# Third PSUM bank, tied inverse products, weight parts in four pieces and the norm behind the next preparation, in a block of RWKV7 and gated attention

## Chip, cores and metric

One core of a Trainium2 chip runs the whole block. Five engines work side by side, each on its own queue of instructions, in order: TensorE multiplies matrices, VectorE and ScalarE work on elements and move results out of PSUM, GpSimd does elementwise work from SBUF, and SyncE issues most of the DMA transfers. The metric is the device time of one execution in microseconds, and less is better.

## What is computed

A sequence of 1024 tokens of width 1024 is normalized and projected; a third of the columns feeds an RWKV7 mixer with 8 heads of 64 (a recurrence over time, a norm of its output per head, a gate), a third feeds causal attention with 8 heads of 64 and a forget bias, and the rest are two gates. Both results are projected, gated, added, projected again, and normalized.

```python
def reference(x, norm_g, w_in, ..., w_out_a, w_out_b, w_out, final_norm_g):
    h = _rmsnorm(x, norm_g[l])
    u = h @ w_in[l]
    u_a, u_b, u_g = jnp.split(u, [RWKV_COLS, RWKV_COLS + FOX_COLS], axis=-1)
    y_a = _rwkv7_mixer(u_a, ...) @ w_out_a[l]
    y_b = _fox_mixer(u_b, ...) @ w_out_b[l]
    g_a, g_b = jnp.split(u_g, 2, axis=-1)
    merged = jax.nn.sigmoid(g_a) * y_a + jax.nn.sigmoid(g_b) * y_b
    x = x + merged @ w_out[l]
    return _rmsnorm(x, final_norm_g)

# in _rwkv7_mixer
    state = (state * w_t[:, :, None, :] + sa[..., None] * b_t[:, :, None, :]
             + v_t[..., None] * k_t[:, :, None, :])          # one step, sa = state @ a_t
    y = (y - mean) * lax.rsqrt(var + LNX_EPS)                # per head
    y = y * lnx_w + lnx_b
    return (y + bonus) * jax.nn.silu(gate)

# in _fox_mixer
    logits = qb @ kp * scale + cum_q - cum_k                 # causal, softmax, times v
    return o * jax.nn.silu(gate)
```

## The kernel before

Every large product is made of three: an operand is split into a part that TensorE's fast fp32 format holds (the H half) and the rest (the L half), and H·H, H·L and L·H are summed. A weight part of 128x1024 is loaded, ScalarE casts it to wH, and GpSimd subtracts, wL = w - wH, in one instruction (split_w, L203 to L206). project (L307 to L313) makes a 128x512 tile of a projection in 8 steps over k of three matmuls each. mix and gate_tile (L322, L351) evacuate such a tile with ScalarE and VectorE: a scaled copy, a shifted combination with the neighbouring token, and the last column kept as last_k and the like.

The program runs through these stages: x is loaded, normalized and transposed (to about 25 us); the projections of r, k, v and of the low-rank inputs for head pairs 0 and 1; then four units, (p, n) = (0,0), (0,1), (1,0), (1,1), each of four heads and half of the sequence. A unit has a preparation, prep, and a chain. prep makes the products of a chunk of 64 tokens (psc, pk and others), inverts triangular matrices by elimination of 32x32 blocks on VectorE (L639, L643, some 30 us), writes them out to DRAM as td and reads them back as Tb, transposes blocks on VectorE (TW, L655), and combines them with two sets of 32 small products on TensorE (pw at L661, pz at L669). chain runs over 8 chunks of time, px, pu and po, with a state that is passed from chunk to chunk, then py (L734) for each four chunks, the norm over the heads (VectorE, L746 to L756), the transposes pt (L761), a scaled copy yo on ScalarE, a product with the gate yg on GpSimd (L771), and a store to yab in DRAM. Behind the four units comes the attention in four pairs of heads: scores sc (L994), softmax on VectorE and ScalarE, transposes pt (L1018), po (L1038). The scores of a pair need qk projected (project_qk), normed and transposed (norm_qk: pqk, pqq, KA, QA), and a copy of parts of QA to other partitions by DMA (L959, L960). At the end merge multiplies y of both mixers by their output weights (pma, pmb) and by the gates.

The order on each engine is made by a list scheduler from priorities: a tile framework takes what was written first unless order(offset) moves its priority. chain and attend run at -LATER, so ahead of all else that is ready. bulky() puts work at +LATER, and that is what fills TensorE meanwhile: the projections of pairs 2 and 3, 24 gate tiles (fill, 48 matmuls of 128x512 each), project_qk, project_v. RFILL, FPRE and FFILL say how many gates may be placed in each of the four units, and ahead of and behind the qk projection in each attention pair. A scheduled order is fixed at build time, and each engine then follows it and waits where an operand is late.

PSUM has eight banks: "pj" 2 (projections), "misc" 2, "aux", "late", "xus" and "y" 1 each (py). Tiles of one tag get its banks in the order in which they are written in the program: a later tile waits until an earlier one has been read, however their priorities stand. ps_misc gives a tile of "misc", ps_pj one of the tags in bulk_tags.

Of the kernel before, what the change touches and what calls it, by code (L numbers as in the profile page):

```python
# [9 lines left out]
F32 = mybir.dt.float32  # L10
# [40 lines left out]
QNB = 1  # L51
QKFIRST = True
LATER = 1000000
PACE = 0.3
PHPOOL = True
APACE = 0
APACE0 = 0.0
FTAGS = ["pj", "pj", "aux"]
TTAGS = ["pj", "misc", "aux", "pj", "misc", "late", "xus"]
PQTAG = ["late", "xus"]  # L60
# [2 lines left out]
NORMPOOL = (0,)  # L63
HSPLIT = 1
HDVE = 0
LSPLIT = 1
PACE0 = 0.0
WA1 = 0
MGB = 3
NQEARLY = True  # L70
ATTFIRST = True
T1B = 3
RFILL = [5, 6, 6, 2]
FPRE = [1, 1, 2, 0]
# [16 lines left out]
def kernel(  # L91
# [6 lines left out]
    nc = tc.nc  # L98
# [9 lines left out]
    bulk_tags = ["pj"]  # L108
# [195 lines left out]
    transposed(1, range(KD))  # L304
    xctx.close()

    def project(ps, wH, wL, rH, rL, n, nk=KD):  # L307

        ts_ = slice(n * HALF, (n + 1) * HALF)
        for k in range(nk):  # L310
            nc.tensor.matmul(ps, wH[:, k, :], rH[:, k, ts_], start=(k == 0), stop=False)  # L311
            nc.tensor.matmul(ps, wH[:, k, :], rL[:, k, ts_], start=False, stop=False)  # L312
            nc.tensor.matmul(ps, wL[:, k, :], rH[:, k, ts_], start=False, stop=(k == nk - 1))  # L313

    yab = dp.tile([8, P, S], F32, tag="yab", name="yab", bufs=1)
    gab = dp.tile([24, P, S], F32, tag="gab", name="gab", bufs=1)
# [76 lines left out]
    HB = 32  # L393
# [84 lines left out]
    def prep(pp_, n):  # L478
# [174 lines left out]
        for e, _, q1, q2 in half:  # L653
            for h in range(2):
                nc.vector.transpose(TW[q1, UC * h : UC * h + UC, :], Tg[q1, h, :, q1])  # L655
        pw = ps_misc(f"pw{u}")
        for h in range(2):
            for c in range(UC):
                g = UC * h + c
                for e, _, q1, q2 in half:  # L660
                    nc.tensor.matmul(pw[q2, g * HB : (g + 1) * HB], Tb[q1, c, h, q2], TW[q1, g, :], start=True, stop=True)  # L661
# [10 lines left out]
        return dict(AR=AR, Q=Q, BKt=BKt, SV=SV, AK=AK, WC=WC, bV=bV, s2c=s2c, lnw=lnw)  # L672

    states = [rp.tile([P, 2, 2, C], F32, tag=f"state{j}", name=f"state{j}") for j in range(2)]
    for t in states:
# [2 lines left out]
    def chain(pp_, n, d):  # L678
# [4 lines left out]
        for c in range(UC):  # L683
            gc = UC * n + c
            st_c, st_n = states[gc % 2], states[1 - gc % 2]
            xs = rp.tile([P, P], F32, tag="xs", name=f"xs{u}_{c}", bufs=2)
            if gc == 0:
                nc.vector.tensor_copy(xs, AK[:, 0])
                nc.gpsimd.memset(yv[:, 0], 0.0)
            else:  # L690

                px = ps_aux(f"px{u}_{c}")
                for e, own, other in pairs:
                    nc.tensor.matmul(
                        px[:, e * P : (e + 1) * P], AR[:, e, c, :], st_c[:, e].rearrange("p h i -> p (h i)"),
                        start=True, stop=True,
                    )
                for e, own, other in pairs:
                    nc.vector.tensor_add(xs[own], px[own, e * P : (e + 1) * P], AK[own, c])
                for e, own, other in pairs:  # L700
                    nc.scalar.copy(yv[own, c].rearrange("p h i -> p (h i)"), px[other, e * P : (e + 1) * P])
                if gc < NCH - 1:
                    ws = rp.tile([P, 2, C], F32, tag="ws", name=f"ws{u}_{c}", bufs=2)
                    for e in range(2):
                        for h, q in ((0, A), (1, B)):
                            nc.scalar.activation(ws[q, e], st_c[q, e, h, :], AF.Copy, scale=WC[q, e, c : c + 1])  # L706
            pu = ps_misc(f"pu{u}_{c}", "late")
            for h in range(2):
                nc.tensor.matmul(pu[:, h * C : (h + 1) * C], Tb[:, c, h, :], xs[:, h * C : (h + 1) * C], start=True, stop=True)
            for e, own, other in pairs:  # L710
                nc.vector.tensor_mul(
                    SV[own, e, c].rearrange("p (h i) -> p h i", h=2),
                    pu[own, 0:P].rearrange("p (h i) -> p h i", h=2),
                    s2c[own, c, :].unsqueeze(2).broadcast_to([64, 2, C]),
                )
            if gc < NCH - 1:
                po = pp.tile([P, HALF], F32, tag="xus", name=f"po{u}_{c}")
                for e, own, other in pairs:
                    nc.tensor.matmul(po[:, e * P : (e + 1) * P], BKt[:, e, c, :], SV[:, e, c, :], start=True, stop=True)
                for e, own, other in pairs:  # L720
                    for h, q in ((0, A), (1, B)):
                        o = po[q, e * P + h * C : e * P + (h + 1) * C]
                        if gc == 0:
                            nc.vector.tensor_scalar(st_n[q, e, h, :], o, WC[q, e, 0:1], None, op0=ALU.mult)
                        else:
                            nc.vector.scalar_tensor_tensor(  # L726
                                st_n[q, e, h, :], o, WC[q, e, c : c + 1], ws[q, e], op0=ALU.mult, op1=ALU.add
                            )
            if c % 4 == 3:
                py = pp.tile([P, HALF], F32, tag="y", name=f"py{u}_{c}").rearrange("p (c h i) -> p c h i", h=2, i=C)  # L730
                for c_ in range(c - 3, c + 1):
                    for h in range(2):
                        for e, own, other in pairs:
                            nc.tensor.matmul(  # L734
                                py[own, c_ % 4, h, :], Q[:, e, h, c_, :], SV[:, e, c_, h * C : (h + 1) * C],
                                start=True, stop=True,
                            )
                yc = yv[:, c - 3 : c + 1]
                nc.vector.tensor_add(yc, yc, py)


        G = 2 * UC
        st = rp.tile([P, 4, G], F32, tag="st", name=f"stat{u}")
        mean, var, rstd, tmp4 = (st[:, j, :] for j in range(4))
# [59 lines left out]
    def project_v(cb):  # L804
# [25 lines left out]
        for b in range(8):  # L830
            bs = slice(b * P, (b + 1) * P)
            pv = ps_pj(f"pfv{cb}_{b}")
            o = pv[:, :ncol]
            for k in range(KD):
                wH, wL = parts[k // KH]
                kk = k % KH
                nc.tensor.matmul(o, hTH[:, k, bs], wH[:, kk, :], start=(k == 0), stop=False)
                nc.tensor.matmul(o, hTH[:, k, bs], wL[:, kk, :], start=False, stop=False)
                nc.tensor.matmul(o, hTL[:, k, bs], wH[:, kk, :], start=False, stop=(k == KD - 1))
# [40 lines left out]
    def project_qk(p):  # L880
# [17 lines left out]
        for n in range(2):  # L898
            xt = fpa[0].tile([P, 4, QB], F32, tag="xn", name=f"xn{p}_{n}", bufs=2)
            rs = fpa[0].tile([P, 3, 16], F32, tag="rs", name=f"rs{p}_{n}", bufs=2)  # L900
            for b in range(4):
                bs = slice((4 * n + b) * P, (4 * n + b + 1) * P)
                ps = ps_pj(f"pf{p}_{n}_{b}")[:, :QB]
                for k in range(KD):
                    wH, wL = parts_[k // KH]
                    kk = k % KH
                    nc.tensor.matmul(ps, hTH[:, k, bs], wH[:, kk, :], start=(k == 0), stop=False)  # L907
                    nc.tensor.matmul(ps, hTH[:, k, bs], wL[:, kk, :], start=False, stop=False)  # L908
                    nc.tensor.matmul(ps, hTL[:, k, bs], wH[:, kk, :], start=False, stop=(k == KD - 1))  # L909
# [14 lines left out]
    def norm_qk(p, xn, rr):  # L924
# [10 lines left out]
        for n in range(2):  # L935
            xg = xn[n].rearrange("p b (g i) -> p (b g) i", i=HD)
            (nc.gpsimd if n in NORMPOOL else nc.vector).tensor_mul(xg, xg, rr[n].unsqueeze(2).broadcast_to([P, 16, HD]))
            for c, key in ((1, "k"), (0, "q")):
# [15 lines left out]
                        )  # L954
                if key == "q":
                    nc.sync.dma_start(qlo[:, HS[n]], ql.bitcast(F32))
            if n == 1:
                QAf = QA.bitcast(F32)
                nc.sync.dma_start(QAf[B, 0, :], QAf[A, 0, :])  # L959
                nc.sync.dma_start(QAf[A, 1, :], QAf[B, 1, :])  # L960
        return KA, QA, qlo, cb

    sc_tags = SCTAGS
# [146 lines left out]
        return mH, mL, [(w[:, 0], w[:, 1]) for w in wo]  # L1110

    units = [(p, n) for p in range(2) for n in range(2)]
    for p in range(2):
        proj_rkv(p)
        if p == 0:
            for p_ in range(NP):
                lora(p_)
    for i, (p, n) in enumerate(units):
        d = prep(p, n)
        if i + 1 == len(units):  # L1120
            open_early()
        with bulky():
            if i == 0:
                proj_rkv(2)
                proj_rkv(3)
            fill(RFILL[i], 0)
            if i + 1 == len(units):
                qk = project_qk(0)
                project_v(0)
                forget()  # L1130
        with order(-LATER):
            chain(p, n, d)
    open_late()
    bulk_tags[:] = FTAGS
    qk = norm_qk(0, *qk)
# [94 lines left out]
```

## Time and profile before

| | |
|---|---|
| median of 3 runs | 1168.89 us (1167.12 to 1171.15) |
| profiled execution, its own time | 1171.96 us |
| its span in the trace | 1170.3 us |
| mean granted clock of TensorE in it | 0.973 |
| TensorE busy | 1064.0 us, 91% of the span |
| VectorE busy | 725.5 us, 62% |
| ScalarE busy | 459.7 us, 39% |
| GpSimd busy | 284.8 us, 24% |

The busy times of the page say which engine is the scarcest. Its idle time is then looked up in the list of waits, which names the instruction that waited and what released it; the timeline of an engine shows a place instruction by instruction; and windows give busy time and granted clock of a stretch, 1.0 being 2.4 GHz and 0.5 being 1.2 GHz. Matmuls overlap in the trace, so the distance of their starts, not their length, says what one costs.

### The profile page before, as it was taken

How to read it: one execution, taken by the hardware profiler on the slowest of the kernel's cores; microseconds unless marked ns; L12 is line 12 of the kernel's file. 1: busy time of each engine (PE TensorE's matmuls, PEld its weight loads, DVE VectorE, ACT ScalarE, POOL GpSimd, SP SyncE). 2: the span in 40 equal slices, each digit the busy share in tenths (PEclk: the TensorE clock that was granted, in tenths of full speed). 3: DMA queues.
4: the chain of work that ended last, by engine and by line, in shares of the span. 5: the costliest groups of instructions: out<-in, count | busy, mean ns of one | idle time of the engine just before them, and what ended most of it. 6: DMA issues, size and time to landing. Idle time of an engine off the chain costs nothing. (4 is left out here: it accounts for less than half of the span.)

```text
span 1170.3 us, 18157 instructions
## 1 busy us (share of the span) xinstructions
PE 1064.0 (91%) x6591; PEld 873.6 (75%) x6591; DVE 725.5 (62%) x1855; ACT 459.7 (39%) x969; POOL 284.8 (24%) x296
## 2 busy tenths in 40 slices
PE   3897998999989898999989979999989788999997
PEld 3676775867768776777888878887968766877886
DVE  7514676588745866386847449686377577466145
ACT  5534232434224331443233346554355355232222
POOL 4420320125110341114201222313222211251400
PEclk9998999999999998999999989999999899999999
DMA  6156434124341343213311151423142150663223
GB/s 207 48 158 211 131 81 114 55 90 123 101 113 46 119 118 108 64 55 83 92 28 38 41 177 42 122 59 91 36 140 86 43 165 19 203 205 114 95 91 126
DMA packets 126043, 118.20 MB, mean 101 GB/s; under 512 B 33361, under 2 KB 91842, under 8 KB 125954
## 3 DMA queue, kind: packets, MB, share of 16 engines
q1 hardware_dynamic: 113664, 94.99, 27.8%
q10 hardware_dynamic: 11714, 21.52, 5.0%
q8 instruction: 52, 0.85, 0.3%
q0 software_dynamic: 576, 0.54, 0.2%
q14 instruction: 37, 0.30, 0.1%
HBM read 79.23 MB, written 35.68 MB: 98 GB/s over the span
## 5 line engine op out<-in xcount | busy, mean ns | idle before, releaser
L311 PE MATMUL ps_gg<-hTH,wH_gg 128*128 128x512 f32 x384 | 158.5, 413 | 3.3 <-DVE gt L338 2.2
L313 PE MATMUL ps_gg<-hTH,wL_gg 128*128 128x512 f32 x384 | 159.4, 415 | 0.0
L312 PE MATMUL ps_gg<-hTL,wH_gg 128*128 128x512 f32 x384 | 157.9, 411 | 0.0
L206 POOL TENSOR_TENSOR wL_gg<-w_gg,wH_gg 128x1024 fp32r<-128x1024 f32 x24 | 60.2, 2508 | 269.6 <-ACT wH_gg L203 263.2
L311 PEld LDWEIGHTS ps_gg<-hTH,wH_gg 128*128 128x128 f32 x384 | 73.4, 191 | 19.3 <-DVE gt L338 3.0
L313 PEld LDWEIGHTS ps_gg<-hTH,wL_gg 128*128 128x128 f32 x384 | 73.9, 192 | 14.6
L312 PEld LDWEIGHTS ps_gg<-hTL,wH_gg 128*128 128x128 f32 x384 | 73.5, 191 | 13.5
L907 PE MATMUL pf<-wqkH,hTH 128*128 128x256 f32 x256 | 74.7, 292 | 0.0
L908 PE MATMUL pf<-wqkL,hTH 128*128 128x256 f32 x256 | 74.7, 292 | 0.0
L909 PE MATMUL pf<-wqkH,hTL 128*128 128x256 f32 x256 | 74.7, 292 | 0.0
L376 ACT ACTIVATE gt<-ps_gg 128x512 f32<-128x512 f32 x40 | 23.9, 598 | 99.9 <-PE ps_gg L313 89.3
L1005 ACT ACTIVATE pr<-pr,mm 128x128 f32<-128x128 f32 (+3 forms) x64 | 49.9, 780 | 28.3 <-DVE mm L1001 27.4
L639 DVE TENSOR_TENSOR etmp<-lt 64x30 f32<-64x30 f32 (+14 forms) x120 | 51.4, 429 | 10.9 <-issue 7.3
L1183 PE MATMUL pz<-wo,mH 128*128 128x512 f32 (+1 forms) x136 | 53.1, 390 | 2.9 <-ACT mH L1092 2.9
L706 ACT ACTIVATE ws<-state,WC 64x64 f32<-64x64 f32 x112 | 38.7, 345 | 40.2 <-DVE state L726 33.5
L1185 PE MATMUL pz<-wo,mL 128*128 128x512 f32 (+1 forms) x136 | 52.6, 387 | 0.0
L1018 PE MATMUL pt<-ident,pr 128*128 128x128 f32 x288 | 48.2, 275 | 4.4 <-DVE pr L1009 4.4
L1184 PE MATMUL pz<-wo,mH 128*128 128x512 f32 (+1 forms) x136 | 52.2, 384 | 0.0
L908 PEld LDWEIGHTS pf<-wqkL,hTH 128*128 128x128 f32 x256 | 49.9, 195 | 0.5
L907 PEld LDWEIGHTS pf<-wqkH,hTH 128*128 128x128 f32 x256 | 49.9, 195 | 0.2
L909 PEld LDWEIGHTS pf<-wqkH,hTL 128*128 128x128 f32 x256 | 49.9, 195 | 0.2
L643 DVE TENSOR_TENSOR lt<-lt,etmp 64x30 f32<-64x30 f32 (+14 forms) x120 | 46.7, 390 | 3.8
(333 smaller groups left out, 2829.5 us busy)
## 6 DMA issues: line engine op xcount, KB each, us to landing
w_gg<-in_w_in_dram SPq DMA_DIRECT2D x24, 512.0 KB, 3.7
gab<-gt ACTq DMA_DIRECT2D x48, 256.0 KB, 2.1
xt<-in_x_dram SPq DMA_DIRECT2D x8, 512.0 KB, 5.8
wqk<-in_w_in_dram SPq DMA_DIRECT2D x16, 256.0 KB, 3.3
cb<-cumd SPq DMA_DIRECT2D x8, 512.0 KB, 5.4
yt<-yab SPq DMA_DIRECT2D x16, 256.0 KB, 3.4
ta<-gab SPq DMA_DIRECT2D x16, 256.0 KB, 3.5
wot<-in_w_out_dram SPq DMA_DIRECT2D x16, 256.0 KB, 2.9
```

The source lines that it names most:

```text
L206: nc.gpsimd.tensor_sub(wL[:, k], w[:, k], wH[:, k])
L311: nc.tensor.matmul(ps, wH[:, k, :], rH[:, k, ts_], start=(k == 0), stop=False)
L312: nc.tensor.matmul(ps, wH[:, k, :], rL[:, k, ts_], start=False, stop=False)
L313: nc.tensor.matmul(ps, wL[:, k, :], rH[:, k, ts_], start=False, stop=(k == nk - 1))
L639: nc.vector.tensor_mul(tm, lt3[:, s, s + 1 :].unsqueeze(1).broadcast_to([4 * NG, s, m]), lt3[:, :s, s].unsqueeze(2).broadcast_to([4 * NG, ...
L907: nc.tensor.matmul(ps, hTH[:, k, bs], wH[:, kk, :], start=(k == 0), stop=False)
L908: nc.tensor.matmul(ps, hTH[:, k, bs], wL[:, kk, :], start=False, stop=False)
L909: nc.tensor.matmul(ps, hTL[:, k, bs], wH[:, kk, :], start=False, stop=(k == KD - 1))
L1005: nc.scalar.activation(pr[:, :w], pr[:, :w], AF.Exp, bias=last, scale=-1.0, accum_out=mm[:, 2:3])
L1183: nc.tensor.matmul(ps, mH[:, k, bs], oH[:, k, c], start=(k == 0), stop=False)
L1184: nc.tensor.matmul(ps, mH[:, k, bs], oL[:, k, c], start=False, stop=False)
L1185: nc.tensor.matmul(ps, mL[:, k, bs], oH[:, k, c], start=False, stop=(k == KD - 1))
```

## The change

Six things change.

1. The norm is taken out of chain and becomes norm_out. It runs at order(LATER // 2) for the first three units and at -LATER for the last.
2. The 32 products pw of each unit are tied by not_before to a place among the projections: laid() counts the third matmul of each step over k, and pw of a unit may stand on TensorE only behind the one with the number in PLACE. The tie orders TensorE's queue and has no semaphore.
3. Projections in the RWKV part have three banks, "pj" twice and "y"; py goes from "y" to "misc", and its 16 products are issued in one block behind the last po or pu of its chunks.
4. A weight part's subtraction on GpSimd is made in four pieces of 128x256 (LSPLIT).
5. The gates move: 20 instead of 19 in the RWKV part, and in the attention pairs 0, 1, 1 and 2 instead of 2, 3, 0 and 0.
6. The copies of QA are made for each half of the sequence (four of 128 KB instead of two of 256 KB).

```diff
-LSPLIT = 1
+LSPLIT = 4
-RFILL = [5, 6, 6, 2]
-FPRE = [1, 1, 2, 0]
-FFILL = [1, 3, 2, 0]
+RFILL = [5, 6, 5, 4]
+FPRE = [0, 0, 1, 2]
+FFILL = [0, 1, 0, 0]
+PLACE = {"pw0_0": 179, "pw0_1": 307, "pw1_0": 424, "pw1_1": 540}
+RTAGS = ["pj", "pj", "y"]
...
+    def laid(ins):
+        laid_.append(ins.ins)
+
+    def not_before(first, name):
+        if name not in PLACE:
+            return
+        for ins in first:
+            tc.add_manual_dep(
+                ins, laid_[PLACE[name]].name,
+                mybir.DependencyInfo(mybir.DependencyClass.NoSync, mybir.DependencyReason.DATA),
+                reason="not_before",
+            )
...
-            nc.tensor.matmul(ps, wL[:, k, :], rH[:, k, ts_], start=False, stop=(k == nk - 1))
+            laid(nc.tensor.matmul(ps, wL[:, k, :], rH[:, k, ts_], start=False, stop=(k == nk - 1)))
...
             if c % 4 == 3:
-                py = pp.tile([P, HALF], F32, tag="y", name=f"py{u}_{c}")...
+                py = pp.tile([P, HALF], F32, tag="misc", name=f"py{u}_{c}", bufs=2)...
+                with tc.issue_after(last_mm.ins):
                     ...
                 nc.vector.tensor_add(yc, yc, py)
+        return yv
+
+    def norm_out(pp_, n, d, yv):
...
-            if n == 1:
-                QAf = QA.bitcast(F32)
-                nc.sync.dma_start(QAf[B, 0, :], QAf[A, 0, :])
-                nc.sync.dma_start(QAf[A, 1, :], QAf[B, 1, :])
+            QAf = QA.bitcast(F32)[:, :, HS[n]]
+            nc.sync.dma_start(QAf[B, 0], QAf[A, 0])
+            nc.sync.dma_start(QAf[A, 1], QAf[B, 1])
...
+    bulk_tags[:] = RTAGS
...
+        not_before(d["pw"], f"pw{p}_{n}")
         with order(-LATER):
-            chain(p, n, d)
+            yv = chain(p, n, d)
+        with order(LATER // 2 if i + 1 < len(units) else -LATER):
+            norm_out(p, n, d, yv)
```

How this moves instructions is shown at three places. The first is TensorE at the end of unit 0's preparation, before. pw are the products on the inverse's blocks, ps_k and ps_r tiles of projections of pairs 2 and 3.

```order
L313 MATMUL ps_k_1627<-hTH,wL_k_1589 128x512
L661 MATMUL pw_0_1308<-TW_0_1303,Tb 32x32
L311 MATMUL ps_k_1627<-hTH,wH_k_1588 128x512
...
L311 MATMUL ps_k_1627<-hTH,wH_k_1588 128x512
L661 MATMUL pw_0_1308<-TW_0_1303,Tb 32x32 x16
L312 MATMUL ps_k_1627<-hTL,wH_k_1588 128x512
...
L661 MATMUL pw_0_1308<-TW_0_1303,Tb 32x32 x15
L311 MATMUL ps_r_1664<-hTH,wH_r_1658 128x512
```

The first product pw stands alone, 13 projection matmuls later follow 16 more and then 15. After the change, at the same place:

```order
L329 MATMUL ps_r_1700<-hTH,wH_r_1691 128x512
L330 MATMUL ps_r_1700<-hTL,wH_r_1691 128x512
L331 MATMUL ps_r_1700<-hTH,wL_r_1692 128x512
L681 MATMUL pw_0_1329<-TW_0_1324,Tb 32x32 x32
L329 MATMUL ps_r_1700<-hTH,wH_r_1691 128x512
L330 MATMUL ps_r_1700<-hTL,wH_r_1691 128x512
```

All 32 stand in one block, and further back: 27 projection matmuls later, counted from pk; in the other units 21, 29 and 4 later.

The second place is TensorE at the end of the last unit, before: py_1_7 is the second half of that unit's y, pcs and pct belong to forget's running sum, pt_1_0 and pt_1_1 are the transposes behind the norm, and sc_0 are the first scores.

```order
L734 MATMUL py_1_7_5913<-SV_1_4608,Q_1_4605 64x64
L838 MATMUL pfv_2_5498<-wvL_0_5425,hTH 128x264
L734 MATMUL py_1_7_5913<-SV_1_4608,Q_1_4605 64x64 x3
L941 MATMUL pqq_0_5999<-ident,xn_0_5162 128x128 x4
...
L866 MATMUL pcs<-lf,tri 128x64
L867 MATMUL pcs<-lf,tri 128x64
...
L875 MATMUL pct<-ident,run 64x128
L761 MATMUL pt_1_0_5954<-ident,yv_1_5706 128x128 x4
...
L761 MATMUL pt_1_1_5961<-ident,yv_1_5706 128x128 x4
...
L994 MATMUL sc_0_0_0_0_6043<-KA_5983,QA_5984 128x256
```

py stood among the values' projections pfv, 160 rows ahead of pcs, and some 125 rows lay between pt and the scores. After the change:

```order
L937 MATMUL pf_0_2_6828<-wqkH_0_6748,hTL 128x256
L903 MATMUL pct<-ident,run 64x128
L758 MATMUL py_1_3_5980<-SV_1_4633,Q_1_4630 64x64 x16
L758 MATMUL py_1_7_6086<-SV_1_4633,Q_1_4630 64x64 x16
...
L935 MATMUL pf_1_2_6958<-wqkH_0_6748,hTH 128x256
L789 MATMUL pt_1_0_6127<-ident,yv_1_5879 128x128 x4
L789 MATMUL pt_1_1_6134<-ident,yv_1_5879 128x128 x4
...
L937 MATMUL pf_1_2_6958<-wqkH_1_6758,hTL 128x256
L969 MATMUL pqk_1_6186<-ident,xn_1_5459 128x128 x4
L969 MATMUL pqq_1_6195<-ident,xn_1_5459 128x128 x4
L1021 MATMUL sc_0_0_0_0_6218<-KA_6156,QA_6157 128x256
```

Both halves of y stand behind pct now, 98 qk matmuls pf lie between them and pt, and pqk, pqq and the scores follow pt by 17 more.

The third place is SyncE's queue ahead of attention 0, before. yab<-yo_1 are the stores of the last unit's output, yg loads of gates, cb the broadcast of the forget sums, QA<-QA the copies that the scores wait for.

```order
L772 DMA yab<-yo_1_5953 128x512
L770 DMA yg_1_1_5972<-gab 128x512
L772 DMA yab<-yo_1_5953 128x512
L821 DMA wv_0_7025<-in_w_in_dram 128x4x256
L976 DMA yg_0_6039<-gab 128x256
L934 DMA cb_5986<-cumd 128x1024 x2
L1052 DMA yt_0_9736<-yab 128x512
L956 DMA qlo_5985<-ql_0_6006 128x512
L959 DMA QA_5984<-QA_5984 64x1024
L960 DMA QA_5984<-QA_5984 64x1024
L973 DMA QZ_0_6033<-qlo_5985 64x256 x2
```

After the change:

```order
L800 DMA yab<-yo_1_6126 128x512
L798 DMA yg_1_1_6145<-gab 128x512
L800 DMA yab<-yo_1_6126 128x512
L1003 DMA yg_0_6214<-gab 128x256
L962 DMA cb_6159<-cumd 128x1024 x2
L986 DMA QA_6157<-QA_6157 64x512
L984 DMA qlo_6158<-ql_0_6179 128x512
L987 DMA QA_6157<-QA_6157 64x512
L986 DMA QA_6157<-QA_6157 64x512
L987 DMA QA_6157<-QA_6157 64x512
```

The copies come in four, and the first still stands behind both stores of yo_1, a load of yg and cb; the load yt of the merge is no longer among them.

## Rows read from the trace of the kernel before

**Rows 1.** The page: busy time, share of the span and instructions of each engine.

```profile
PE 1064.0 (91%) x6591; PEld 873.6 (75%) x6591; DVE 725.5 (62%) x1855; ACT 459.7 (39%) x969; POOL 284.8 (24%) x296
```

**Rows 2.** TensorE's waits: line <- what it waited for: total us, times, longest.

```profile
PE pw L661 <- DVE TW L655: 14.9, 4, 4.2
...
PE ps_r L311 <- DVE last_k L344: 8.6, 2, 5.2
...
PE sc L994 <- DMA QA<-QA: 7.0, 2, 6.2
...
PE pt L761 <- DVE yv L756: 5.3, 3, 3.1
...
PE pma L312 <- DVE ya L1054: 4.1, 3, 1.8
...
PE pma L311 <- ACT ya L1053: 3.0, 1, 3.0
...
PE pv L506 <- DVE bon L609: 2.3, 1, 2.3
```

**Rows 3.** Windows: length; busy PE, PEld, DVE, ACT, POOL; granted clock; DMA share; GB/s.

```profile
99.00:111.00 12.00, 6.76 (x17) 5.12 (x18) 5.00 (x11) 4.28 (x7) 2.36 (x1) 0.72 0.48 176
...
457.00:470.00 13.00, 8.77 (x56) 6.13 (x54) 3.00 (x6) 1.53 (x2) 0.68 (x1) 0.74 0.58 151
...
692.20:752.50 60.30, 58.57 (x382) 51.32 (x383) 44.32 (x132) 32.91 (x81) 16.93 (x30) 0.96 0.29 88
...
925.00:945.30 20.30, 13.25 (x44) 9.58 (x43) 16.31 (x30) 10.58 (x18) 2.64 (x1) 0.75 0.43 131
...
945.30:999.90 54.60, 47.89 (x281) 37.44 (x280) 41.64 (x120) 28.61 (x70) 11.55 (x23) 1.00 0.25 82
```

**Rows 4.** Timeline of TensorE around pw of unit 0: start, length, instruction, wait ahead.

```profile
190.91 0.40 PE L312 MATMUL ps_k<-hTL,wH_k 128*128 128x512 f32 x1
...
191.14 0.40 PE L313 MATMUL ps_k<-hTH,wL_k 128*128 128x512 f32 x1
...
195.20 0.24 PE L661 MATMUL pw<-TW,Tb 32*32 32x32 f32 x2 [3.66 <-DVE TW L655]
...
196.54 0.63 PE L311 MATMUL ps_k<-hTH,wH_k 128*128 128x512 f32 x1
...
196.97 0.63 PE L312 MATMUL ps_k<-hTL,wH_k 128*128 128x512 f32 x1
```

**Rows 5.** Timeline of VectorE, end of unit 0's elimination, same columns.

```profile
184.29 2.36 DVE L639 TENSOR_TENSOR etmp<-lt 64x108 f32<-64x108 f32 x1
...
186.69 0.26 DVE L643 TENSOR_TENSOR lt<-lt,etmp 64x108 f32<-64x108 f32 x1
...
194.71 0.43 DVE L655 STREAM_TRANSPOSE TW<-Tb 32x256 f32<-32x256 f32 x1 [0.63 <-DMA Tb<-td]
```

**Rows 6.** GpSimd: one weight part in the timeline; a group (busy, mean ns, idle before).

```profile
184.13 2.40 POOL L206 TENSOR_TENSOR wL_v<-w_v,wH_v 128x1024 fp32r<-128x1024 f32 x1 [10.33 <-ACT wH_v L203]
...
L1042 POOL TENSOR_TENSOR yo<-yo,yg 128x256 f32<-128x256 f32 x16 | 14.5, 908 | 36.3 <-DVE yo L1041 35.4 <-POOL QZ L972 0.9
```

**Rows 7.** Timeline of SyncE's queue ahead of attention 0: issue, length, transfer.

```profile
677.24 0.32 SPq L772 DMA_DIRECT2D yab<-yo  x1
...
683.52 1.25 SPq L959 DMA_DIRECT2D QA<-QA  x1
```

**Rows 8.** Timeline of VectorE, norm of the last unit: its first and last operations.

```profile
640.02 0.69 DVE L739 TENSOR_TENSOR yv<-yv,py 128x512 f32<-128x512 f32 x1 [0.36 <-PE py L734]
...
651.36 1.22 DVE L756 TENSOR_TENSOR yv<-yv,bV 128x1024 f32<-128x1024 f32 x1
```

**Rows 9.** Timeline of TensorE, last unit's pt and qk matmuls behind it.

```profile
667.70 0.66 PE L761 MATMUL pt<-ident,yv 128*128 128x128 f32 x4 [1.00 <-ACT cT L877]
...
672.86 0.28 PE L907 MATMUL pf<-wqkH,hTH 128*128 128x256 f32 x1
...
672.98 0.28 PE L908 MATMUL pf<-wqkL,hTH 128*128 128x256 f32 x1
```

More of the change, by code (lines that the diff above doesn't have):

```diff
@@ L305 @@
     xctx.close()
+    laid_ = []
+    def laid(ins):
[9 more added lines that the diff above has]
+            )
     def project(ps, wH, wL, rH, rL, n, nk=KD):
@@ L656, in prep @@
         pw = ps_misc(f"pw{u}")
+        mms = []
         for h in range(2):
@@ L660, in prep @@
                 for e, _, q1, q2 in half:
-                    nc.tensor.matmul(pw[q2, g * HB : (g + 1) * HB], Tb[q1, c, h, q2], TW[q1, g, :], start=True, stop=True)
+                    mms.append(
+                        nc.tensor.matmul(
+                            pw[q2, g * HB : (g + 1) * HB], Tb[q1, c, h, q2], TW[q1, g, :], start=True, stop=True
+                        ).ins
+                    )
         for e, _, q1, q2 in half:
@@ L671, in prep @@
             nc.scalar.copy(Tg[q1, :, :, q2], pz[q1, :].rearrange("p (h c t) -> p h c t", h=2, t=HB))
-        return dict(AR=AR, Q=Q, BKt=BKt, SV=SV, AK=AK, WC=WC, bV=bV, s2c=s2c, lnw=lnw)
+        return dict(AR=AR, Q=Q, BKt=BKt, SV=SV, AK=AK, WC=WC, bV=bV, s2c=s2c, lnw=lnw, pw=mms)
     states = [rp.tile([P, 2, 2, C], F32, tag=f"state{j}", name=f"state{j}") for j in range(2)]
@@ L708, in chain @@
             for h in range(2):
-                nc.tensor.matmul(pu[:, h * C : (h + 1) * C], Tb[:, c, h, :], xs[:, h * C : (h + 1) * C], start=True, stop=True)
+                last_mm = nc.tensor.matmul(pu[:, h * C : (h + 1) * C], Tb[:, c, h, :], xs[:, h * C : (h + 1) * C], start=True, stop=True)
             for e, own, other in pairs:
@@ L718, in chain @@
                 for e, own, other in pairs:
-                    nc.tensor.matmul(po[:, e * P : (e + 1) * P], BKt[:, e, c, :], SV[:, e, c, :], start=True, stop=True)
+                    last_mm = nc.tensor.matmul(po[:, e * P : (e + 1) * P], BKt[:, e, c, :], SV[:, e, c, :], start=True, stop=True)
                 for e, own, other in pairs:
@@ L729, in chain @@
             if c % 4 == 3:
[L730 to L737, printed above, removed]
+                py = pp.tile([P, HALF], F32, tag="misc", name=f"py{u}_{c}", bufs=2).rearrange("p (c h i) -> p c h i", h=2, i=C)
+                with tc.issue_after(last_mm.ins):
+                    for c_ in range(c - 3, c + 1):
+                        for h in range(2):
+                            for e, own, other in pairs:
+                                nc.tensor.matmul(
+                                    py[own, c_ % 4, h, :], Q[:, e, h, c_, :], SV[:, e, c_, h * C : (h + 1) * C],
+                                    start=True, stop=True,
+                                )
                 yc = yv[:, c - 3 : c + 1]
                 nc.vector.tensor_add(yc, yc, py)
+        return yv
+    def norm_out(pp_, n, d, yv):
+        u = f"{pp_}_{n}"
         G = 2 * UC
@@ L838, in project_v @@
                 nc.tensor.matmul(o, hTH[:, k, bs], wL[:, kk, :], start=False, stop=False)
-                nc.tensor.matmul(o, hTL[:, k, bs], wH[:, kk, :], start=False, stop=(k == KD - 1))
+                laid(nc.tensor.matmul(o, hTL[:, k, bs], wH[:, kk, :], start=False, stop=(k == KD - 1)))
             pvv = pv[:, 0:256].rearrange("p (g h i) -> p g h i", g=2, h=2)
@@ L908, in project_qk @@
                     nc.tensor.matmul(ps, hTH[:, k, bs], wL[:, kk, :], start=False, stop=False)
-                    nc.tensor.matmul(ps, hTL[:, k, bs], wH[:, kk, :], start=False, stop=(k == KD - 1))
+                    laid(nc.tensor.matmul(ps, hTL[:, k, bs], wH[:, kk, :], start=False, stop=(k == KD - 1)))
                 nc.scalar.copy(xt[:, b], ps)
```

## Prediction

> **What bounds the kernel now.** I read the page's busy times first: TensorE is busy 1064.0 of 1170.3 us, VectorE 725.5, all others less [rows 1]. So TensorE sets the end, and time can come only from its 106 us of idle and from stretches in which it runs at half its clock. The list of what TensorE waited for comes next [rows 2]: in it four waits for VectorE's transposes ahead of pw (one in each unit's preparation) cost 14.9 us, two waits for last_k 8.6 us, the wait for the copied q ahead of the first scores 7.0 us, and the merge's waits for ya 7.1 us. Then I read the granted clock in windows [rows 3]: it falls where TensorE had just stood idle for some 3 to 6 us. Between 457 and 470 us it is 0.74, over 13 us a loss of 3.4 us. Behind unit 0's pw, which waited 3.66 us, projection matmuls follow each other at 0.43 us instead of 0.23 [rows 4], the lower of the clock's two levels (1.2 for 2.4 GHz), for about 3.4 us, a loss of 1.7. Each long wait has therefore a second price of 1.7 to 3.4 us behind it. The last thing read is what makes pw late: td goes out and Tb comes back, the transposes end only after that, and the elimination ahead of them contains operations that stand still beside a GpSimd subtraction [rows 5].
>
> The profiled execution took 1171.96 us, of which 1170.3 is its span, and stands 3.07 us above the median of 1168.89. All sums below are made against 1171.96, and 3.07 is taken off at the end.
>
> **The third bank for projections.** Before, a projection's fifth and later tiles wait until one of two banks is evacuated. The longest such wait is 5.2 us at 99.8 us, with another of 3.4 (8.6 in two) [rows 2], and the clock is at 0.72 over the 12 us that follow, 3.4 us lost [rows 3]. With three banks ps_r finds a free one. The evacuation itself (one ScalarE and two VectorE operations) isn't faster, so a later tile may still wait a little: from 8.6 + 3.4 I take **12**, bounds 6 and 13.
>
> **The tied products, the inversion.** The kernel's order was 1 + 16 + 15 products pw between projections; now they stand as one block of 32, and counted in the new order pw comes 27, 21, 29 and 4 projection matmuls later in the four units. At 0.23 us from one such matmul to the next [rows 4] that is 6.2, 4.8, 6.7 and 0.9 us. Against this the block needs all four transposes, not the first alone, which end 1 to 1.5 us behind the first, and TensorE arrives earlier, since the waits for banks ahead of it (about 2.1 us in unit 0, 1.4 in unit 1) go as well. Compared from the end of the products that precede the elimination: in unit 0 the transposes end after 40.5 us and TensorE reaches pw after 39.0; in unit 1 43.7 against 42.5; in unit 2 35.7 against 36.4; in unit 3 some 35 to 38 against 33.2. So waits of 3.66, 3.2, 4.2 and 3.8 us (14.9 in all) become at most 1.5, 1.2, 0 and 3, if the elimination takes as long as before. Together with the clock behind them (1.7 + 1.7 + 3.4 + 1.7 = 8.5) and the banks (3.5) 26.9 us are at stake. I take **22**, bounds 8 and 27. Who pays for the later pw is the chain, which stands behind pw and pz; it hides behind projections as long as there are any, and the planned gates grow from 19 to 20 in this part, so it isn't late here.
>
> **The weight parts in four pieces.** One 128x1024 subtraction on GpSimd took 2.40 us [rows 6]. It began at 184.13, and a VectorE operation that began at 184.29 lasted 2.36 us, while its like of the same 64x108 shape took 0.26 [rows 5]: 2.1 us lost, on the path to pw. I count about 35 such. What four pieces of 128x256 do isn't in this trace. Nearest is a 128x256 product on GpSimd, 0.91 us mean [rows 6]. If a held operation is let go after one piece and the next piece holds none, the loss falls from 2.1 to 0.9 and each subtraction beside an elimination gives back 1.2; if every piece holds one, four of 0.91 make 3.6 instead of 2.4, and each costs 1.2 more. Three to an inversion: between 3.6 us less and 3.6 us more. I take 1.5 us less, nearer to the first end, because beside GpSimd's shorter products, which also run one behind another, I find no VectorE operation that stands still through several of them. It removes the remainders of 1.5 and 1.2 above and gives nothing further, as TensorE then waits for nothing there.
> The page "SBUF — State Buffer" of the Trainium skill (section "Who interferes with whom") says that a VectorE instruction with two SBUF inputs contends with a GpSimd instruction that reads SBUF, and that the later one blocks completely until the first ends. The 2.36 us against 0.26 [rows 5] agree; by this rule alone every piece would take the pair anew, and the worse end, 3.6 us more in each inversion, would be the value.
>
> **The norm.** Its code now stands behind the next preparation, but in the planned order its transposes pt still come ahead of the next unit's first products in units 0 to 2, with 72, 65 and 62 projection matmuls between py and pt instead of 73, 66 and 64. So for these the edit doesn't do what it says, and the waits of pt for yv, 5.3 us in three [rows 2], shrink only by the shorter VectorE work: **2** with the clock behind. The other small waits of chain 0 and preparation 1, mainly pv's for bon, 2.3 [rows 2], with the clock drop behind it, give **4.5**; those of chain 3 and of the values' projections **2.5**.
>
> **The last unit's y.** Moving py from a bank of its own to the two "misc" banks costs. forget() is written ahead of chain 3, so its pct comes first in those banks; both py blocks of unit 3 stand behind pct, and so does the norm. From the last addition of py (640.02) to the end of the norm's last operation (652.58) it is 12.6 us [rows 8], the two blocks and additions add about 2. TensorE has 98 qk matmuls of 0.12 us [rows 9] to fill that, 11.6 us, so pt waits 1 to 3. Behind pt the chain to the first scores was, before: pt's last at 668.36 [rows 9], the second yab issued at 677.24, the copy of q at 683.52 [rows 7], its data 7 to 9 us later. Before, that was covered by some 125 qk and gate matmuls and still left 6.2 us [rows 2]. Now pqk and the scores follow pt by 17 matmuls, 2 us, plus 1 us of transposes. SyncE's queue has the same yab, yg, yab, yg, cb ahead of QA, and the yab stores wait for GpSimd's product: from pt to QA about 11.5 us, and with the first half of q alone copied 3 to 5.5 more, 14.5 to 17. Idle 11 to 14 us instead of 1.0 + 6.2, the wait of pt on top, and a longer time at half clock: **-10**, bounds -4 and -16.
>
> **The gates taken out of attention.** Attention 0 took 60.3 us, with 58.57 of TensorE's busy time in it [rows 3]; 25.4 us of that were other products, and 11.7 remain. The nearest case is attention 3, with 15.0 us of other products: 54.6 us, 47.89 busy, 6.7 idle at full clock [rows 3]. With 11.7 I take 10 idle instead of 1.7: **-8**, bounds -3 and -14. Attention 1 loses some filling (21.8 to 18.7) but gains its gates' waits elsewhere: **-1.5**; attentions 2 and 3 start a little later for the copies behind yab: **-0.5**.
>
> **The merge.** Before, pma stood ahead of attention 3 and waited for ya, 4.1 + 3.0 us [rows 2], at a clock of 0.75 over the 20.3 us from 925 [rows 3], 5.1 us lost; attention 3 then idled 6.7. Two gates now stand there, and ya is made beside attention 3's end. From 7.1 + 5.1 + some of the idle: **+12**, bounds 6 and 18.
>
> **Sum.** 12 + 22 + 2 + 4.5 + 2.5 - 10 - 8 - 1.5 - 0.5 + 12 = 35. 1171.96 - 35 = 1137; less 3.07, **1134 us**.
>
> **Rivals.** *Full gain*: the late y and the thin attention 0 cost little (-4 and -3), because the first half of q is copied early and VectorE does the scores' work without TensorE's queue in its way. Then 1134 - 6 - 5 - 2 (attentions 1 to 3) = 1121, and with inversions at their bound of 27, 1116. For it: VectorE is busy only 44 us in attention 0 [rows 3]. Against: the chain of SyncE, GpSimd and DMA behind pt is in the trace.
> *The pieces hold as long as one*: the eliminations take up to 3.6 us more, pw waits and the clock falls as before, and only the banks' 3.5 of the 22 remain: 1134 + 18.5 = 1152. For it: GpSimd runs the four pieces one behind another. The rule of the SBUF page leads to this case.
> *Slower*: attention 0, so thin, is granted 1.2 GHz all through. At that level matmuls followed each other at 0.43 instead of 0.23 to 0.24 us [rows 4], some 0.83 of their time more. With 45 us of TensorE's work in attention 0 and 25 more at attention 1's start that costs 58: 1134 + 58 = 1192. It decides from 46 us of work at the low clock (38 / 0.83, 38 being 1172 - 1134). For it: the idle 11 us ahead of the first scores, and attention 0 is at 0.96 already [rows 3]. Against: attention 3, with 6.7 us idle, ran at 1.00 [rows 3].
>
> **How the numbers follow.** The forecast 0.55, full gain 0.22, the pieces 0.16, slower 0.05, the rest other. A difference within 0.3% (3.5 us) is about what a measurement of this kernel can tell from none. The forecast's own bounds are 1122 to 1148; for 8 in 10 the range takes in most of the full gain and of the pieces: 1112 to 1154. Faster by over 0.3%: 0.91; within: 0.04; slower: 0.05.
>
> **What would show it.** In the trace after: no wait for last_k over 1 us near 100 us; pw's four waits under 5 us together; clock at full in the inversions; the first scores waiting 11 us and more for QA, with pt behind pct; attention 0 with about 10 us idle; pma without waits for ya. It is wrong if VectorE's eliminations last longer than the 30 us before, if the clock stays down in attention 0, or if SyncE serves QA ahead of yab.

## The result and the profile after

The changed kernel takes 1138.79 us (median of 4, 1133.43 to 1140.04) against 1170.02 of the kernel before (4 runs measured with it); the ratio is 0.9722, 95% interval 0.9679 to 0.9765. The profiled execution took 1139.32 us, its span is 1137.6. Forecast were 1134 us and a gain of 35; the two profiled executions differ by 32.6.

The page's busy times of the changed kernel, as in [rows 1]:

```profile
PE 1054.3 (93%) x6591; PEld 870.0 (76%) x6591; DVE 712.9 (63%) x1855; ACT 458.6 (40%) x969; POOL 316.6 (28%) x467
```

TensorE's idle time in the span fell from 106 to 83 us; its busy time fell too, by 10 us, with as many matmuls. The mean granted clock is almost the same (0.974 against 0.973), so the clock isn't what most of these 10 us come from; what is stays open. The waits of TensorE, as in [rows 2]:

```profile
PE sc L1021 <- DMA QA<-QA: 9.0, 1, 9.0
...
PE pt L789 <- DVE yv L784: 6.5, 4, 2.3
...
PE psc L583 <- DVE BK L574: 3.5, 3, 2.6
...
PE ps_r L329 <- DVE last_k L362: 2.5, 1, 2.5
...
PE pma L329 <- ACT ya L1080: 1.7, 1, 1.7
...
PE pw L681 <- DVE TW L673: 0.6, 2, 0.4
...
PE pma L330 <- DVE ya L1081: 0.5, 2, 0.3
...
PE pv L524 <- DVE bV L633: 0.4, 1, 0.4
```

The waits of pw have shrunk from 14.9 to 0.6 us, that for last_k is 2.5 instead of 8.6, pma waits 2.2 instead of 7.1. psc waits 3.5 us for BK instead of 0.8, and the scores wait longer than before. Windows, as in [rows 3]; the third is attention 0 up to the first scores of attention 1:

```profile
100.00:112.00 12.00, 9.47 (x35) 7.30 (x34) 4.59 (x12) 5.56 (x8) 2.81 (x4) 0.86 0.63 206
...
505.00:523.00 18.00, 15.38 (x63) 13.16 (x62) 7.77 (x11) 1.91 (x5) 8.96 (x13) 0.62 0.28 69
...
662.50:731.80 69.30, 58.11 (x350) 48.52 (x350) 49.32 (x141) 36.25 (x87) 14.93 (x36) 0.88 0.24 74
...
889.60:956.90 67.30, 60.04 (x335) 47.59 (x335) 51.59 (x135) 38.40 (x86) 18.46 (x37) 0.97 0.34 104
```

To see where time went I cut the span at the first products of each unit's preparation (pss), at the first pu of its chain, and at the first scores of each attention pair. What a stage lost is its length less its products' own time, each shape at the distance of starts that it has at full clock. By this estimate all products together need 946.4 us in both kernels; 223.9 us were lost before, 191.2 after. Taken with the median distance of each shape the products need some 40 us more, and both kernels lose that much less; the column of gains changes by at most 0.5 us, so the gains can be relied on and the losses themselves are rough.

| stage | lost before | lost after | gain | forecast |
|---|---|---|---|---|
| start to pss of unit 0 | 37.3 | 28.8 | 8.5 | 12 |
| preparations of units 0, 1, 2 | 50.0 | 23.3 | 26.7 | 22.5 |
| preparation of unit 3 | 14.3 | 15.7 | -1.4 | 4 |
| chains of units 0, 1, 2 | 30.8 | 27.0 | 3.8 | 2 |
| chain of unit 3 to the first scores | 24.7 | 24.9 | -0.2 | 2.5 - 10 |
| attention 0 | 9.8 | 27.5 | -17.7 | -8 |
| attention 1 | 11.9 | 6.7 | 5.2 | -1.5 |
| attentions 2 and 3, first pma | 30.9 | 28.2 | 2.7 | 12 - 0.5 |
| output products pz | 14.1 | 9.2 | 4.9 | 0 |

(The forecast's 22 for the inversions and 4.5 for preparation 1 are split over the second and third line, 4 of them in unit 3.) The total was right to 3 us, but four lines missed by 7 to 10 us each, to both sides, and made up for one another: that it came out so near is luck.

### The profile page after: what moved, and what is told of

It is laid out like the page before. It is cut to its first block, busy times and chain, and to the rows that moved or that the text cites. A ratio compares the mean times of both kernels' runs of the same rounds, so it can differ in the third digit from the quotient of the medians.

```text
span 1137.6 us, 18393 instructions
## 1 busy us (share of the span) xinstructions
PE 1054.3 (93%) x6591; PEld 870.0 (76%) x6591; DVE 712.9 (63%) x1855; ACT 458.6 (40%) x969; POOL 316.6 (28%) x467
## 5 line engine op out<-in xcount | busy, mean ns | idle before, releaser
L208 POOL TENSOR_TENSOR wL_gg<-w_gg,wH_gg 128x256 fp32r<-128x256 f32 x96 | 72.2, 782 | 227.9 <-ACT wH_gg L205 224.7
L1045 PE MATMUL pt<-ident,pr 128*128 128x128 f32 x288 | 51.4, 288 | 7.7 <-DVE pr L1036 7.6
L657 DVE TENSOR_TENSOR etmp<-lt 64x30 f32<-64x30 f32 (+14 forms) x120 | 46.3, 386 | 11.4 <-issue 7.7
L1028 DVE CUSTOM_DVE_ANT_0 pr<-sc,cb 128x128 f32<-128x128 f32 (+3 forms) x64 | 33.9, 535 | 30.0 <-PE sc L1026 17.0
```

What stands on the lines that cost most here:

```text
L208: nc.gpsimd.tensor_sub(wL[:, k], w[:, k], wH[:, k])
L1045: nc.tensor.transpose(pt[:, o : o + P], probs[e][:, kb * P : (kb + 1) * P], ident)
```

## Experiments

Two theories of the gain in the units: A, the tie of pw and the third bank give it; B, the weight parts in pieces do, by a shorter elimination.

**The pieces taken back.**

```diff
-LSPLIT = 4
+LSPLIT = 1
```

> The changed kernel with a weight part's subtraction in one piece again. In the trace of the changed kernel a VectorE operation beside a piece of 128x256 lasts 0.43 us longer than its like, four in a row 1.7 us, against 2.1 us beside the whole part. Theory A (the pieces are not what shortened the inversion; tie and bank are): 1136 to 1143 us, pw waits under 3 us in all, the elimination at most 1.5 us longer. Theory B (the pieces gave the gain of the inversions): 1150 to 1158, with pw waits of 8 us and more.

Measured: 1143.85 us (1138.83 to 1152.85, 6 runs), ratio 0.9784, 0.9751 to 0.9817. That is some 5 us slower than the change, with intervals that overlap: a little above theory A's range and far from B's, with 1.2 us of waiting at pw. So the pieces aren't what most of the gain rests on. By the stages of the table, unit 0's preparation lost 7.6 us more, and unit 3's lost 6.7 less; the profiled execution (1139.84 us) was one of the two fastest, so it tells where time moved and not how much in all.

**The pieces alone, in the kernel before.**

```diff
-LSPLIT = 1
+LSPLIT = 4
```

> The kernel before, with the subtraction in four pieces and nothing else. Theory A: pw still waits 12 to 16 us in four, and the time is within 5 us of the kernel before (1165 to 1172). Theory B: the pieces take 6 us and more from the inversions and their low clock, 1155 to 1160.

Measured: 1155.63 us (6 runs), ratio 0.9883, 0.986 to 0.9906, a gain of 13.5 us: as large as B said, in a way that neither theory had. Busy times and two waits of this kernel:

```profile
PE 1063.7 (92%) x6591; PEld 874.4 (76%) x6591; DVE 708.6 (61%) x1855; ACT 459.9 (40%) x969; POOL 321.4 (28%) x467
```

```profile
PE pw L661 <- DVE TW L655: 12.2, 4, 3.7
...
PE pt L761 <- DVE yv L756: 1.9, 3, 1.4
```

pw still waits 12.2 us, so the inversions gave only part. Of the 16.9 us between the two profiled spans 5.9 lie in the four preparations, 9.0 in the four chains and 2.6 at the start. The norm on VectorE had been held by weight parts as well. The same operation of it beside a weight part, before and with pieces:

```profile
256.96 3.40 DVE L754 TENSOR_TENSOR yv<-yv,stat 128x1024 f32<-128x1024 f32 x1
```

```profile
251.44 1.73 DVE L754 TENSOR_TENSOR yv<-yv,stat 128x1024 f32<-128x1024 f32 x1
```

Alone it takes 1.23 us. pt's wait for yv fell from 5.3 [rows 2] to 1.9, and VectorE was busy 17 us less (725.5 in [rows 1]).

**Without the tie.**

```diff
-PLACE = {"pw0_0": 179, "pw0_1": 307, "pw1_0": 424, "pw1_1": 540}
+PLACE = {}
```

> The changed kernel without the tie of pw to a place: pw stands where the scheduler puts it, as 1 + 16 + 15 products. Theory A (the tie is what removes the waits for the transposes): pw waits 10 to 15 us in four and TensorE falls to half speed behind them for 3 to 7 us each, so 1152 to 1162. Rival (the third bank and the pieces had removed most of it; the tie only moves work): pw waits under 6 us, 1139 to 1147.

Measured: 1152.53 us, ratio 0.9853, 0.9834 to 0.9873, as theory A said. The waits:

```profile
PE pw L681 <- DVE TW L673: 17.4, 4, 5.2
```

Units 0, 1 and 2 lost 7.7, 6.5 and 9.6 us more; unit 3 lost 5.9 less. Even with the pieces, then, the transposes are late unless pw stands further back.

**Two banks.**

```diff
-RTAGS = ["pj", "pj", "y"]
+RTAGS = ["pj"]
```

> The changed kernel with two banks for projections in the RWKV part (py stays in the misc banks). Theory A: the waits for evacuation come back, 5 us and a half-speed stretch near 100 us and 1 to 2 us in each of the first two inversions, 1148 to 1156. Rival (the gain at the start came from elsewhere, the pieces or the order): 1138 to 1144.

Measured: 1151.21 us (1148.89 to 1156.93), ratio 0.9847, 0.9814 to 0.9881, as theory A said. TensorE's timeline near 100 us shows the old wait:

```profile
105.49 0.77 PE L329 MATMUL ps_r<-hTH,wH_r 128*128 128x512 f32 x1 [5.03 <-DVE last_k L362]
```

The start lost 9.3 us more, the preparations of units 0 and 1 2.0 and 4.6.

**Two theories of attention 0**, which lost 17.7 us more than before: C, it lacks filling; D, the wait ahead of the first scores and the low clock behind it do it.

**Two gates into attention 0, out of unit 3.**

```diff
-RFILL = [5, 6, 5, 4]
-FPRE = [0, 0, 1, 2]
-FFILL = [0, 1, 0, 0]
+RFILL = [5, 6, 5, 2]
+FPRE = [1, 0, 1, 2]
+FFILL = [1, 1, 0, 0]
```

> The changed kernel with two gate tiles moved from the last unit to attention 0 (as many as stood there before). In the changed kernel attention 0 took 69 us with 42 of work, 20 idle and 17 at half speed. Theory C (attention 0 lacks filling): its loss falls by 7 to 10, 1129 to 1133. Rival D (the loss comes from the wait of 9 us ahead of the first scores and from the low clock behind it): the same time within 3 us, 1136 to 1142.

Measured: 1122.71 us, ratio 0.9593, 0.9564 to 0.9622, better than C had it. Attention 0, and the place that the gates left in unit 3:

```profile
648.60:712.90 64.30, 59.80 (x400) 50.31 (x398) 51.52 (x146) 38.67 (x95) 17.96 (x40) 1.00 0.33 100
```

```profile
553.96 0.58 PE L935 MATMUL pf<-wqkH,hTH 128*128 128x256 f32 x1 [6.81 <-ACT sq L940]
```

Attention 0 runs at full clock and loses 11.3. The stage ahead of it loses 10.1 less too: with the two gates gone the scheduler puts some 110 products between pt and the first scores where 20 had been, and these no longer wait for QA. So the run speaks for C and D at once. The price is a wait of 6.8 us in unit 3's preparation.

**forget() behind the norm.**

```diff
                 project_v(0)
-                forget()
...
             norm_out(p, n, d, yv)
+        if i + 1 == len(units):
+            with order(LATER):
+                forget()
```

> The changed kernel with forget() written behind chain and norm of the last unit, so that py doesn't stand behind pct in the misc banks. Theory D: the first scores wait for the copied q under 2 us instead of 9, the stretch of 13.7 us at half speed ahead of and in attention 0 goes, 1124 to 1131. Rival C (filling is what lacks, the wait only moves into attention 0): 1136 to 1142.

Measured: 1114.58 us (1113.33 to 1116.32), ratio 0.9529, 0.9503 to 0.9555. This is below D's range, and more than D's share: py no longer stands behind pct. TensorE at the end of the last unit's chain, in the change and here:

```profile
598.70 0.66 PE L732 MATMUL pu<-xs,Tb 128*128 128x64 f32 x4
...
630.96 0.27 PE L903 MATMUL pct<-ident,run 128*64 128x128 f32 x1
631.16 2.09 PE L758 MATMUL py<-SV,Q 128*64 128x64 f32 x64
```

```profile
595.17 0.66 PE L732 MATMUL pu<-xs,Tb 128*128 128x64 f32 x4
595.76 1.22 PE L758 MATMUL py<-SV,Q 128*64 128x64 f32 x32
```

In the change the last pu is done 32 us before py starts, right behind pct; here py follows at once. So norm and pt are done while the values are projected, and most of pair 1's qk products, which had been used up in waiting for the norm, are left for attention 0. Its products' own time is 54.7 us instead of 41.8. Its window:

```profile
635.80:706.50 70.70, 61.81 (x462) 55.70 (x460) 52.17 (x160) 41.19 (x102) 19.28 (x41) 1.00 0.27 81
```

The clock is full, against 0.88 in the change. The stage ahead of attention 0 lost 10.7 us less, attention 0 11.4 less.

**Both.** forget() behind the norm and the two gates moved.

> Both edits: two gates in attention 0 and forget() behind the norm. If the two causes are separate, the gains add: 1117 to 1125. If one of them carried all, it is as good as the better of the two and no more, 1126 to 1132.

Measured: 1123.16 us, ratio 0.9593, 0.9562 to 0.9625: the gains don't add, and it is worse than forget() alone. The time lies in the range forecast for gains that add, but that range had been made before the two were measured: alone they gave 16 and 24 us, and added up these would have made some 1099 us. Unit 3's preparation, without its two gates, lost 27.5 us instead of 15.7; its clock was low for 27.7 us.

**The old places of the gates in the changed kernel.**

```diff
-RFILL = [5, 6, 5, 4]
-FPRE = [0, 0, 1, 2]
-FFILL = [0, 1, 0, 0]
+RFILL = [5, 6, 6, 2]
+FPRE = [1, 1, 2, 0]
+FFILL = [1, 3, 2, 0]
```

> The changed kernel with the gates placed by the old tables (5, 6, 6, 2 in the units, 1, 1, 2, 0 and 1, 3, 2, 0 in attention). If the new places of the gates are a gain, as the prediction's merge term of 12 us says, this is slower, 1142 to 1150. If filling in attention 0 is worth more than the merge, as the changed kernel with two gates moved there (1122.7) suggests, it is faster, 1122 to 1134, with the merge's waits for ya back (5 us and more at low clock ahead of attention 3) and attention 0 without its 17 us loss.

Measured: 1123.92 us, ratio 0.9593, 0.9562 to 0.9624. The new places of the gates cost 15 us in all. What they give at the end is seen in the waits that come back with the old ones (pma 4.3 us, where 5 and more had been expected):

```profile
PE pz L1214 <- ACT mH L1119: 4.0, 1, 4.0
...
PE pma L329 <- ACT ya L1080: 3.0, 1, 3.0
...
PE pma L330 <- DVE ya L1081: 1.3, 3, 0.7
```

The output products lost 5.9 us more with the old places, attentions 2 and 3 with the first pma some 2.7 more; attention 0 and the stage ahead lost 15.6 and 8.8 less.

**The norm at the chain's priority.**

```diff
-        with order(LATER // 2 if i + 1 < len(units) else -LATER):
+        with order(-LATER):
```

> The changed kernel with the norm at the chain's priority for all four units, as before. In the planned order pt then moves by three projection matmuls in the first unit. Theory (the norm's new priority does nothing): within 4 us of the changed kernel, 1135 to 1143. Rival (it keeps VectorE free for the next preparation): 1145 to 1152, with later psc.

Measured: 1133.0 us (1131.07 to 1143.82), ratio 0.9683, 0.963 to 0.9737, which overlaps the change's interval: no loss from undoing the norm's move, if anything a gain of a few us. The rival's loss of 6 us and more is excluded.

**Towards a better version**: three kernels, all with forget() behind the norm. In the first the gates of attentions 1 and 2 are moved to attention 0, in the second the weight parts come in two pieces instead of four, in the third one gate is moved.

```diff
-FPRE = [0, 0, 1, 2]
-FFILL = [0, 1, 0, 0]
+FPRE = [1, 0, 0, 2]
+FFILL = [1, 0, 0, 0]
```

> The changed kernel with forget() behind the norm (1114.6 us alone), and the gates of attentions 1 and 2 moved to attention 0. Attention 0 lost 16 us in that kernel and attentions 1 and 2 lost 7 and 13. If filling is still what attention 0 lacks, 1108 to 1112; if its rest is bound by VectorE and ScalarE, the gates only leave holes in attentions 1 and 2, 1115 to 1122.

```diff
-LSPLIT = 4
+LSPLIT = 2
```

> The changed kernel with forget() behind the norm and the weight parts in two pieces. With four, one 128x512 operation of VectorE in unit 3 stood through all four pieces (3.03 us) and TensorE ran at half speed for 10 to 14 us behind the wait. If two pieces of some 1.25 us each hold as 0.43 times their number in short ones, they cost less in a row but more in the chains: 1112 to 1118, no clear difference. If long pieces hold a chain's operation whole, 1118 to 1124.

```diff
-FPRE = [0, 0, 1, 2]
-FFILL = [0, 1, 0, 0]
+FPRE = [1, 0, 0, 2]
+FFILL = [0, 1, 0, 0]
```

> The changed kernel with forget() behind the norm and one gate moved, from attention 2 to attention 0 (attention 1 keeps its own). With both gates in attention 0 the time was 1110.3, with none 1114.6: attention 0 gained 5 us by them, attentions 2 and 3 together 7, and attention 1 without its gate lost 9. If these are separate, this keeps most gains without that loss: 1103 to 1108. If a gate in attention 1 is worth nothing and the loss there belongs to the shifted order, 1109 to 1114.

Measured, in this order: 1110.28 us (ratio 0.9462, 0.9427 to 0.9497), 1112.62 (0.9498, 0.9465 to 0.953) and 1113.26 (0.9518, 0.9496 to 0.954). The first is the fastest kernel here, 61 us below the one before in the same measurement. From forget() alone (1114.58) it is 4 us away, and of the three only its interval stands just apart. The one-gate kernel missed its forecast of 1103 to 1108: attention 1 lost 5.6 us less than with both gates moved, but attention 0 lost 3.5 and attention 3 4.6 more. Two pieces can't be told from four.

## Why the prediction was right, and where it wasn't

**TensorE as the bound, and the tie: right.** TensorE was to reach pw 39.0, 42.5, 36.4 and 33.2 us behind pk; it did so after 38.6, 42.1, 36.0 and 32.8, each 0.4 earlier. At unit 0, as in [rows 4]:

```profile
185.49 0.39 PE L331 MATMUL ps_r<-hTH,wL_r 128*128 128x512 f32 x1
185.81 1.20 PE L681 MATMUL pw<-TW,Tb 32*32 32x32 f32 x64
```

All of pw (64 matmuls in the trace) stands in one block, with no wait ahead. The run without the tie shows that it carried this, 13.7 us by the medians; in units 0 to 2 the preparations gave 26.7 us where 22.5 were forecast.

**The third bank: right in mechanism, size 8.5 instead of 12** at the start, since 2.5 of the 8.6 us of waiting for last_k remained, where under 1 had been forecast; with what it saves in units 0 and 1, two banks cost 12.4 us.

**The pieces: the size taken was near, the reason and the place were wrong.** VectorE beside four pieces, and GpSimd's four pieces there:

```profile
174.12 0.70 DVE L657 TENSOR_TENSOR etmp<-lt 64x108 f32<-64x108 f32 x1
174.86 0.69 DVE L661 TENSOR_TENSOR lt<-lt,etmp 64x108 f32<-64x108 f32 x1
175.59 0.67 DVE L657 TENSOR_TENSOR etmp<-lt 64x84 f32<-64x84 f32 x1
176.29 0.66 DVE L661 TENSOR_TENSOR lt<-lt,etmp 64x84 f32<-64x84 f32 x1
176.99 0.21 DVE L657 TENSOR_TENSOR etmp<-lt 64x58 f32<-64x58 f32 x1
```

```profile
173.97 2.89 POOL L208 TENSOR_TENSOR wL_v<-w_v,wH_v 128x256 fp32r<-128x256 f32 x4 [8.17 <-ACT wH_v L205]
```

Each piece holds one operation, as the worse end of the prediction had it, but for 0.70 us instead of 0.26 only, since the operation ends just behind its piece and a piece is 0.72 us. Four lose 1.7 us where one whole part lost 2.1 [rows 5]: 0.4 us back for each subtraction, 1.2 for three in an inversion, where I took 1.5. The page "SBUF — State Buffer" of the Trainium skill (section "Who interferes with whom") says that the later instruction blocks until the first ends. These rows agree with it piece by piece; BK in unit 3 below, which stands through three pieces that began after it, does not. The 3.6 us more that I drew from it don't follow: by the rule as well, what is lost is the piece less the operation's own time. And I put the gain into the inversions alone, where the tie made it worth little; in the old kernel the pieces gave 13.5 us, somewhat over half of it in the chains, where the norm runs.

**Unit 3: wrong by 5 us, for a wait that I hadn't priced.** There a 128x512 operation of VectorE (0.75 us elsewhere) isn't let in between the pieces but stands through all four. VectorE, then TensorE behind it:

```profile
505.21 3.03 DVE L569 SCALAR_TENSOR_TENSOR BK<-bx,col,Ei 128x512 f32<-128x512 f32 x1 [1.02 <-PE pb L595]
```

```profile
509.42 3.75 PE L583 MATMUL psc<-AR,BK 64*128 64x128 f32 x16 [2.62 <-DVE BK L574]
...
513.82 3.78 PE L583 MATMUL psc<-AR,BK 64*128 64x128 f32 x16
```

BK is late, psc waits 2.62 us, TensorE falls to 1.2 GHz, and the two sets of psc that follow run at it: 13.7 us low, clock 0.62 over the 18 us from 505. With one piece psc waited 1.3 us there and the stage lost 9.0; without the tie, where it waited 0.4 at this place, 9.8; with two pieces 15.5, as much as with four. With the norm at the chain's priority the weight part came a little later, and the next operation (L574, also 128x512) was held instead (3.83 us, 0.7 to 1.1 elsewhere). So the collision hangs on when a weight part arrives; that pieces as such bring it isn't shown. Why BK isn't let in stays open, for others are: a 128x512 operation of unit 1 (AR, 0.75 us elsewhere) took 1.31 beside pieces.

**The norm: right that its move does nothing, not shown in what it forecast for the waits.** Undoing the move costs nothing that can be measured. But pt's waits for yv in units 0 to 2 didn't shrink: they are 5.6 us instead of 5.3. The chains gained 3.8 us where 2 were forecast, and by what isn't shown.

**The last unit's y: mechanism and time right, size wrong.** From pt's end to the first scores 14.5 to 17 us were forecast; it is 15.4, with yab, yg and cb ahead of QA in SyncE's queue. TensorE, and that queue, as in [rows 7]:

```profile
646.08 1.06 PE L789 MATMUL pt<-ident,yv 128*128 128x128 f32 x8 [0.84 <-DVE yv L784]
...
662.52 0.77 PE L1021 MATMUL sc<-KA,QA 128*128 128x256 f32 x2 [8.99 <-DMA QA<-QA]
```

```profile
653.98 0.32 SPq L800 DMA_DIRECT2D yab<-yo  x1
...
656.37 0.48 SPq L986 DMA_DIRECT2D QA<-QA  x1
```

Idle between pt and the scores with pt's own wait is 12.4 us against 7.2 before, a loss of 5 where I had 10: the clock was low from 652.4 us on, and TensorE stood idle from 653.5 anyway. By difference, the rest of that stage gave some 5 us back.

**Attention 0: the term was mis-sized, 17.7 instead of 8.** The idle time was nearly right (11.2 us within it, 10 forecast). What failed is "6.7 idle at full clock" [rows 3] as the nearest case: attention 0 started at the low clock and fell to it three more times, 17.2 us in all against 5.2, an estimated 6 us lost. With 9 us more of idle time that makes 15 of the 17.7; the rest is open. The rival of the clock was thus true in part. And the two terms, late y and thin attention, weren't separate: the qk products of pair 1 that filled the wait for the norm are those that attention 0 then lacked. forget() behind the norm gave both back, 24 us.

**Attention 1 and the merge: wrong by 7 and 9, opposite signs.** Attention 1 gained 5.2 by itself: the waits for xn (2.8 us) and pr (2.2) that stood in it are gone. The merge's waits went as forecast (7.1 to 2.2 us), but the clock, for which 5.1 were counted, gave 1.7 (low for 6.8 us in attentions 2 and 3 instead of 10.2), and attention 3 with two gates still idled 7.3 us (6.7 before). New waits there, for xn (3.6 us in two) and QZ (3.2 in two), took most of the gain back, so that of 11.5 only 2.7 came. At the output products, where I forecast nothing, 4.9 us came: pz's 2.9 us wait and the clock behind it are gone; with the old places of the gates it waits 4.0 us again.

**The gates** as a whole, which I had as -8 and +12, cost 15 us: the old places in the changed kernel are that much faster. The sign of this part of the change was wrong.

## What to carry to other kernels

When products are moved to fill a hole, ask which stage they are taken from and whether it has another filling: two gates moved to attention 0 were worth 16 us in the changed kernel, where it lacked filling, and 4 once forget() had left it other products. A PSUM ring in program order is a queue like any engine's: a tile written early for late work (pct) held back the tiles of urgent work (py) and cost 24 us, and one moved line of code gave it back. Where a serial chain on one engine meets long instructions of a neighbour, cutting those is worth trying first: it was one line, and 13.5 us alone, though only some 5, with intervals that overlap, beside the tie and the third bank.

## What the runs showed of the hardware beyond expectation

A VectorE operation beside back-to-back GpSimd pieces behaved in two ways. Most took turns with them: 64x108 ones (0.70 us each instead of 0.26), 128x1024 ones of the norm (1.64 to 1.73 instead of 1.23), a 128x512 one (1.31 instead of 0.75). But in one place, in unit 3, a 128x512 operation stood through all four (3.03 us instead of 0.75), and did so again in most of the runs on the changed kernel; size alone doesn't tell which will. Four pieces took GpSimd 2.8 to 2.9 us against 2.40 for the whole part. Behind a wait of 2.6 us TensorE stayed at 1.2 GHz for 10 to 14 us where small products (psc, 64 rows) came next, and for 3.4 us behind pw's 3.66 us [rows 4] or pt's 2.3, where 128x512 ones came next; behind pw's 4.2 us in unit 2 of the kernel before, with 128x512 ones next, it was 6.8.

Not tried: the copies of QA for each half of the sequence by themselves, and py in a bank of its own beside a third one for projections, for which the eight banks don't suffice.
